# Attention in units of four query tiles, V's scalings and low parts on VectorE, and weights split in three scheduled steps

## The chip, the cores and the metric

The kernel runs on one core of one Trainium2 chip. The metric is the device time of one execution in microseconds (us). The core has TensorE (PE, matrix products and transposes; PEld is its weight load), VectorE (DVE), ScalarE (ACT), GpSimd (POOL) and SyncE (SP, which issues most DMAs). Each engine executes its own instruction list in the order in which the program holds it; semaphores join the lists. Data live in SBUF (128 partitions), sums of matmuls in PSUM banks of 128x512 fp32.

## The reference

The model has two pre-RMSNorm layers on x of 1024 tokens by 1024 features, all float32. Layer 0 is a gated DeltaNet and a gated ConvFFN. Then one K and one V are projected from the stream, and layer 1 is chunked softmax attention on them and a second ConvFFN.

```python
h = h + gated_deltanet(rmsnorm(h, a_norm[0]), ...)
h = h + conv_ffn(rmsnorm(h, f_norm[0]), ...)
kv = rmsnorm(h, kv_norm) @ w_kv                  # 1024 x 2048, K and V of 16 heads of 64
h = h + chunk_attention(rmsnorm(h, b_norm[0]), b_w_q[0], b_rel_bias[0], b_w_out[0], k_pad, v_pad)
h = h + conv_ffn(rmsnorm(h, f_norm[1]), ...)
return rmsnorm(h, final_norm)

def one_chunk(args):                             # 64 queries against a band of 9 chunks of 64 keys
    s = jnp.einsum("bqhd,bkhd->bhqk", q_n, k_band) * scale + bias
    s = jnp.where(valid, s, NEG_INF)
    p = jax.nn.softmax(s, axis=-1)
    return jnp.einsum("bhqk,bkhd->bqhd", p, v_band)
```

## The kernel before

Every fp32 operand of a product is held as a high part (fp32r, `...h` or `whi`) and a low part (what is left, `...l` or `wlo`), and a product is three matmuls: high by high, low by high, high by low (`dense`, L118 to L120). So each operand costs a cast to the high part, mostly on ACT, and a subtraction for the low part, on POOL or DVE.

The program has these stages, in us of the profiled execution: the DeltaNet layer to about 690, FFN 0 to about 1300, the norm and the projection of V to 1411, attention to 1895, FFN 1 to the end. The FFNs and V's projection save matmuls with a scheme of seven products for eight blocks (numbered 1 to 7), whose operands are sums of blocks; each needs its own cast (`uh`, ACT) and subtraction (`ul`).

**The FFN's tail.** Up products go to the PSUM tile `pul`; `vpre`, `gate` and `val` (L1690 to L1696) are the convolution and the gate, `hidh`/`hidl` their product in two parts, `pf` the down product, whose weights are `fr`, `fh` and `fl`. V's weights, tiles `v` of 128x512, are loaded here by SP (L2244).

**V's projection** is `first_halves` with the inner `values()`. Its order is written by hand: `seq` is the list of products and each helper job is put at a place of that list with a rank (`at(i, f, rank)`); the list of every engine follows from it. `fold` scales a tile `v` by the norm's gain (`colt`), `sums` and `left_sum` make the sums of blocks, on the side of the activations (`h`) and of the weights (`v<-v,v`), `highs`/`lows` split the former into `xsum`, `operand` splits the latter into `uh`/`ul`, `product` is 12 matmuls to `pv` (L1475 to L1477), `after` adds products up to `vsum`. The helper `tt` records every `tensor_tensor` there under one line, L1400. Operands of a product are prepared two places ahead of it. The norm ahead of this, `norm_steps`, multiplies `h` by the broadcast factor `psb` (L390), casts `xh` (L393) and subtracts `xl` (L381).

**Attention.** 16 heads are eight pairs p of two heads a; a query tile is 128 queries, a key tile 128 keys, and a query tile sees up to five key tiles (640 keys). For a pair, `kv_tile` projects k and q from weights that are folded (POOL), cast (ACT `whi`, L101) and subtracted (POOL `wlo`, L103); `post_k`, `post_q` and `turn_halves` make the tiles `kA`, `qA`, `qL` and `V`, which hold high and low parts together. Then for one query tile `score` (PE `sc`, L2445/L2446; DVE L2450 adds the bias and finds the maximum; ACT exp L2454; DVE reciprocal L2458; POOL division L2460) leaves the shares `sS`; `turn_run` transposes them (`ptp`, L2505) and splits them into `pTh` (ACT, L2518) and `pTl` (DVE, L2525); `apply_run` multiplies by V into `poT` (L2550/L2551), and the two halves of `poT` are added (ACT `tm` L2556, DVE `oT` L2561). A unit is one head and two query tiles, 64 of them. The out-projection is `acco`.

The order of all engines in attention is made when the program is built, by the list scheduler `Flow` (object `wv`). It keeps a clock T of PE, adds estimated costs of the other engines (`on("D"|"A"|"G", cost)`), and takes at each step the first item by rank whose inputs are ready by that clock; where none is, it places one step of dense work (three matmuls of the next projection, `_dense`). `fetch` loads and splits weights of dense tiles ahead.

Of the kernel before, what the change touches and what calls it, by code (L numbers as in the profile page):

```python
# [9 lines left out]
F32 = mybir.dt.float32  # L10
# [18 lines left out]
def trunk_kernel(  # L29
# [168 lines left out]
    class Flow(Weave):  # L198
# [4 lines left out]
        def __init__(self):  # L203
            super().__init__()
            self.T, self.free, self.aux = 0.0, dict(D=0.0, A=0.0, G=0.0), deque([[0.0], [0.0]])
            self.time, self.items, self.last, self.stalls = {}, [], 0, []
            self.auto, self.tick, self.slack, self.cur, self.nxt, self.units = True, 0, 0.5, None, deque(), 0
            self.brief, self.early, self.split_at, self.hold, self.far = False, 8, 8, None, 4.0

# [60 lines left out]
        def _dense(self):  # L270
            if self.cur is None:
# [3 lines left out]
                if self.nxt[0][1] < 2:  # L275
                    self.stalls.append(self.T)
                    self.T += 3.0 + max(0.0, self.nxt[0][2] + 6.0 - self.T)
                    self.fetch(2)
                e = self.nxt.popleft()
# [69 lines left out]
    def norm_steps(h, s, g, dst, keep=False, gap=False):  # L349
# [29 lines left out]
        def low(t_, k):  # L379
            eng = (nc.gpsimd if k in (0, 1, 2, 3) else nc.vector) if keep and s == 1 else (nc.vector if k % 2 == 0 else nc.gpsimd)  # L380
# [1016 lines left out]
    def values(wts, pss, raw, load, fh, fin, wf, wd, d_vt, more):  # L1397
# [40 lines left out]
        def fold(j, q):  # L1438
# [3 lines left out]
            tt(nc.gpsimd, t_, t_, g, ALU.mult)  # L1442
# [14 lines left out]
        def operand(j, n):  # L1457
# [4 lines left out]
            tt(nc.gpsimd, lo, src, hi.bitcast(F32), sub)  # L1462
# [96 lines left out]
    def ffn(layer, h, hp, xs, tail, d_r, last):  # L1559
# [475 lines left out]
        if layer == 0:  # L2035
# [16 lines left out]
            def closing(s, m):  # L2052
                def f():
                    tt(nc.vector, fh[m][:, hs(s)], fps[s, m], fh[m][:, hs(s)], add)
                    nc.sync.dma_start(out=d_h[m][:, hs(s)], in_=fh[m][:, hs(s)])
                    if m == 0:
                        norms.append(norm_steps(fh, s, None, last, keep=True))
# [229 lines left out]
    with ExitStack() as ph:  # L2287
# [19 lines left out]
        wv.far = 5.79  # L2307

        def kv_tile(src, c0, g, post):
# [5 lines left out]
            wt = split_w(raw, shape, fold=g)  # L2315
            wv.on("G", 3.61, wv.on("A", 0.89, wv.on("G", 2.6)))
# [92 lines left out]
        def bias_tile(hd):  # L2409

            b = bp.tile([P, 640], F32, name="bt", tag="bt", bufs=3)
# [21 lines left out]
        def score(u, kv, a, t, bt):  # L2433
# [14 lines left out]
            S = bp.tile([P, n, w], F32, name="sS", tag="sS", bufs=6)  # L2448
# [17 lines left out]
        units = [(p, *((i % 2, i // 2) if p == 7 else (i // 4, i % 4))) for p in range(8) for i in range(8)]  # L2466
        oTs = {}

        def score_run():
            for p, a, tp in units:  # L2470
# [5 lines left out]
                for i in range(2):  # L2476
                    while live[0] >= 6:
# [4 lines left out]
                    sc.append(score(("S", p, a, tp, i), kvs[p], a, 2 * tp + i, bt))  # L2482
                    yield
                shares.append(sc)
                wv.mark(("sc", p, a, tp), sc_free[0])
                if (a, tp) == (1, 3):
                    wv.mark(("scored", p), sc_free[0])

        def turn_run():
            for p, a, tp in units:  # L2490
                yield from wait(("sc", p, a, tp), *[("S", p, a, tp, i) for i in range(2)])
                sc = shares.popleft()
                kt0, kt1 = sc[0][1], 2 * tp + 1
                blocks = [((kt, 0), (kt, 1)) for kt in range(sc[1][1], 2 * tp + 1)]
                blocks.append(((kt0, 0) if sc[1][1] > kt0 else None, (kt1, 1)))
                for b0 in range(0, len(blocks), 2):
                    bl = blocks[b0 : b0 + 2]
# [3 lines left out]
                    pt = pB.tile([P, 2, 256], F32, name="ptp", tag="pt", bufs=2)  # L2501
                    some = [(j, e) for j, b in enumerate(bl) for e in b if e is not None]
                    for j, e in some:
                        S, s0 = sc[e[1]]
                        nc.tensor.transpose(pt[:, j, e[1] * P : (e[1] + 1) * P], S[:, (e[0] - s0) * P : (e[0] - s0 + 1) * P], ident)  # L2505
                    wv.pe(len(some), 0.15)
                    if b0 + 2 >= len(blocks):
                        live[0] -= 2
                    pTh = bp.tile([P, 2, 256], F32R, name="pTh", tag="pTh", bufs=3)
                    pTl = bp.tile([P, 2, 256], F32R, name="pTl", tag="pTl", bufs=3)  # L2510
                    if bl[-1][0] is None:
                        v = [(0, slice(0, 256)), (1, slice(P, 256))] if len(bl) == 2 else [(0, slice(P, 256))]
                        v = [(pt[:, j, c], pTh[:, j, c], pTl[:, j, c]) for j, c in v]
                    else:
                        n = len(bl)
                        v = [(pt[:, 0:n], pTh[:, 0:n], pTl[:, 0:n])]
                    for s_, h_, l_ in v:
                        nc.scalar.copy(h_, s_)  # L2518
                    t0 = wv.on("A", 0.2 * len(v) + 0.1 * len(some))
                    one = [None, p, a, tp, b0, bl, b0 + 2 >= len(blocks), pTh, pTl]  # L2520
                    pts.append(one)

                    def low(v=v, one=one, slot=slot, n=len(some)):
                        for s_, h_, l_ in v:
                            nc.vector.tensor_tensor(l_, s_, h_.bitcast(F32), op=ALU.subtract)  # L2525
                        one[0] = slot[0] = wv.on("D", 0.08 * len(v) + 0.135 * n)
# [4 lines left out]
        def apply_run():  # L2531
            left = sum(1 for _ in units)
# [343 lines left out]
```

## Time and profile before

| | |
|---|---|
| time, median of 2 runs | 2560.38 us (2556.89 and 2563.86) |
| the profiled execution | 2561.97 us, span 2560.3 us |
| mean granted TensorE clock | 0.991 |
| busy: PE, DVE, ACT, POOL | 2488.0, 1885.7, 1466.9, 1550.6 us |
| 1238 to 1312 (tail of FFN 0): PE busy, clock | 68.41 of 74.00 us, 0.95 |
| 1338 to 1411 (V's products): PE, DVE, POOL busy, clock | 65.30, 36.44, 64.00 of 73.00 us, 0.95 |
| 1472 to 1728 (attention, middle): PE, DVE, ACT, POOL busy, clock | 241.06, 181.21, 172.14, 113.25 of 256.00 us, 0.95 |

A row of a timeline is start, duration, engine, line, operation, result<-inputs, shapes and, in brackets, how long the engine idled before it and what ended that. A row of a group is count, busy time and mean duration in ns, then the idle time of the engine before such instructions. Matmuls overlap, so the time of one is read from the distance of two starts. Half clock shows as starts that lie twice as far apart and as a clock under 1.00.

### The profile page before, as it was taken

The page shows a single profiled execution, that of the slowest core. Times are in us where ns is not written, and L with a number is a line of the kernel's source. Part 1 is how long each engine was busy: PE and PEld are TensorE (multiplying, and loading weights), DVE is VectorE, ACT ScalarE, POOL GpSimd, SP SyncE. Part 2 cuts the span into 40 slices and gives each one's busy share as a digit, 9 for nine tenths or more (in the row PEclk, how much of TensorE's full clock was granted, in tenths as well). Part 3 has the DMA queues.
Part 4 walks back from the last instruction along what each step waited for, and adds up shares of the span by engine and source line. Part 5 has one row for each costly group of instructions (what it writes and reads, how often), then busy time and mean ns, then how long its engine had stood idle before and what let it go on. Part 6 is the DMA issues. An engine that isn't in the chain of part 4 may idle for free.

```text
span 2560.3 us, 39405 instructions
## 1 busy us (share of the span) xinstructions
PE 2488.0 (97%) x13741; PEld 2064.4 (81%) x13741; DVE 1885.7 (74%) x3036; ACT 1466.9 (57%) x2824; POOL 1550.6 (61%) x1533
## 2 busy tenths in 40 slices
PE   8999999999999999999989999999999999999998
PEld 6888888888788888887777788888877887888877
DVE  5765774466888888888674566777579788888886
ACT  6444646554565565655455566666455655666555
POOL 3655553358267777777438444445462777787775
PEclk9999999999999999999999999999999999999999
DMA  8734444555357776668932322222253689877788
GB/s 224 181 107 130 123 130 151 156 176 168 85 121 152 153 145 140 139 142 185 226 97 50 88 57 57 74 60 82 97 157 100 170 158 187 165 168 169 157 185 223
DMA packets 388168, 354.26 MB, mean 138 GB/s; under 512 B 101888, under 2 KB 308736, under 8 KB 387968
## 3 DMA queue, kind: packets, MB, share of 16 engines
q1 hardware_dynamic: 354992, 244.51, 34.0%
q0 software_dynamic: 28224, 98.58, 21.8%
q10 hardware_dynamic: 4752, 8.65, 0.9%
q8 instruction: 108, 1.77, 0.3%
q14 instruction: 92, 0.75, 0.1%
HBM read 182.25 MB, written 156.83 MB: 132 GB/s over the span
## 4 chain that ended last, share of the span: by engine, by line
PE 72%; POOL 7%; DVE 6%; issue 5%; DMA 5%; ACT 2%; SPq 1%; ACTq 0%; POOLq 0%; DVEq 0%
PE pu L1600 7%; PE acc L118 7%; PE acc L119 7%; PE pu L1598 7%; PE pu L1599 7%; PE acc L120 6%; POOL ul L1564 3%; PE pd L1598 3%; PE pd L1600 3%; PE pd L1599 3%; DMA d_rt<-rm 2%; PE acco L118 2%; PE acco L120 2%; PE acco L119 2%; PE ptp L2505 2%
## 5 line engine op out<-in xcount | busy, mean ns | idle before, releaser
L1564 POOL TENSOR_TENSOR ul<-r,uh 128x512 fp32r<-128x512 f32 x266 | 430.2, 1637 | 254.6 <-ACT uh L1586 251.5
L118 PE MATMUL acc<-xh,whi 128*128 128x512 f32 x800 | 333.6, 417 | 0.4 <-ACT xh L1094 0.4
L119 PE MATMUL acc<-xl,whi 128*128 128x512 f32 x800 | 316.2, 395 | 1.7 <-POOL xl L381 1.6
L120 PE MATMUL acc<-xh,wlo 128*128 128x512 f32 x800 | 315.3, 394 | 0.0
L1586 ACT CAST uh<-r 128x512 fp32r<-128x512 f32 x289 | 177.0, 622 | 189.9 <-DVE r L1564 149.8
L103 POOL TENSOR_TENSOR wlo<-wraw,whi 128x256 fp32r<-128x256 f32 (+1 forms) x294 | 216.1, 766 | 99.3 <-ACT whi L101 97.9
L1600 PE MATMUL pu<-xh,ul 128*128 128x512 f32 x524 | 204.7, 391 | 1.7 <-POOL ul L1564 1.7
L1598 PE MATMUL pu<-xh,uh 128*128 128x512 f32 x524 | 204.5, 390 | 0.8 <-ACT keep L1727 0.7
L1954 ACT COPY stage<-pd 128x1024 f32<-128x1024 f32 x180 | 175.3, 1013 | 51.3 <-PE pd L1600 48.7
L1599 PE MATMUL pu<-xl,uh 128*128 128x512 f32 x524 | 204.0, 389 | 0.0
L2460 POOL TENSOR_SCALAR sS<-sS,st 128x640 f32<-128x640 f32 (+4 forms) x128 | 88.0, 691 | 178.3 <-DVE st L2458 146.2
L1693 DVE SCALAR_TENSOR_TENSOR gate<-gpre,colt,gate 128x1023 f32<-128x1023 f32 (+2 forms) x92 | 173.4, 1885 | 11.4 <-ACT gate L1690 10.7
L1564 POOL TENSOR_TENSOR dl<-a,dh 128x512 fp32r<-128x512 f32 x90 | 153.3, 1704 | 46.2 <-ACT dh L1586 37.2
L120 PEld LDWEIGHTS acc<-xh,wlo 128*128 128x128 f32 x800 | 151.4, 189 | 33.4
L119 PEld LDWEIGHTS acc<-xl,whi 128*128 128x128 f32 x800 | 152.4, 191 | 27.0 <-POOL xl L381 4.1
L118 PEld LDWEIGHTS acc<-xh,whi 128*128 128x128 f32 x800 | 152.2, 190 | 24.1 <-ACT xh L1094 0.8
L1693 DVE SCALAR_TENSOR_TENSOR val<-vpre,colt,val 128x1023 f32<-128x1023 f32 x88 | 146.9, 1670 | 33.3 <-ACT val L1690 33.2
L1564 DVE TENSOR_TENSOR r<-r,r 128x512 f32<-128x512 f32 x160 | 130.8, 817 | 35.1 <-POOL ul L1564 33.9
L2450 DVE CUSTOM_DVE_ANT_0 sS<-sc,bt 128x640 f32<-128x640 f32 (+4 forms) x128 | 83.9, 656 | 74.3 <-PE sc L2446 62.8
L1600 PEld LDWEIGHTS pu<-xh,ul 128*128 128x128 f32 x524 | 98.3, 188 | 24.8 <-POOL ul L1564 3.4
L1564 DVE TENSOR_TENSOR el<-val,eh 128x512 fp32r<-128x512 f32 x90 | 86.7, 963 | 43.0 <-ACT eh L1586 43.0
L1598 PEld LDWEIGHTS pu<-xh,uh 128*128 128x128 f32 x524 | 98.4, 188 | 21.7 <-ACT keep L1727 1.1
(456 smaller groups left out, 7504.9 us busy)
## 6 DMA issues: line engine op xcount, KB each, us to landing
r<-in_f_w_up_dram SPq DMA_DIRECT2D x176, 256.0 KB, 4.7
d_r<-stage POOLq DMA_DIRECT2D x78, 512.0 KB, 8.1
d_c<-stage POOLq DMA_DIRECT2D x70, 512.0 KB, 8.6
a<-in_f_w_down_dram SPq DMA_DIRECT2D x72, 256.0 KB, 2.9
wraw<-in_a_w_in_dram SPq DMA_DIRECT2D x32, 512.0 KB, 4.5
d_e<-stage POOLq DMA_DIRECT2D x32, 512.0 KB, 8.6
wraw<-in_a_w_out_dram SPq DMA_DIRECT2D x16, 512.0 KB, 4.2
d_r<-h ACTq DMA_DIRECT2D x32, 256.0 KB, 3.0
```

Of the source, the lines that this page charges most:

```text
L103: nc.gpsimd.tensor_tensor(lo[:, c], raw[:, c], hi[:, c].bitcast(F32), op=ALU.subtract)
L118: mm(ps, hi[:, kw, wcol : wcol + P], rh[k][s], start=st, stop=False)
L119: mm(ps, hi[:, kw, wcol : wcol + P], rl[k][s], start=False, stop=False)
L120: mm(ps, lo[:, kw, wcol : wcol + P], rh[k][s], start=False, stop=sp)
L1564: tt = lambda eng, o, a, b, op: eng.tensor_tensor(o, a, b, op=op)
L1586: copy(hi, src)
L1598: mm(ps, w[0][:, cw], x[0], start=first, stop=False, skip_group_check=True)
L1599: mm(ps, w[0][:, cw], x[1], start=False, stop=False, skip_group_check=True)
L1600: mm(ps, w[1][:, cw], x[0], start=False, stop=last, skip_group_check=True)
L1693: nc.vector.scalar_tensor_tensor(t_[:, a:c1], p_[:, a - step : c1 - step], w[:, 2 - step : 3 - step], t_[:, a:c1], op0=ALU.mult, op1=ALU.add)
L1954: nc.scalar.copy(t_, ps)
L2460: nc.gpsimd.tensor_scalar(S, S, st[:, 3:4], 1.0, op0=ALU.mult, op1=ALU.mult)
```

## The change

1. `norm_steps` gets `odd=True` for the last norm of layer 0: for half 1 the low parts of even tiles are made on DVE and of odd ones on POOL, instead of tiles 0 to 3 on POOL and the rest on DVE.
2. In `values()` the 12 `fold` and the 21 `ul` of `operand` go from POOL to DVE, and the places of `sums`, `highs`, `lows` and `fold` in the list are other ones. The first fold, which stands in the FFN's tail, goes with them.
3. A unit of attention is one head and four query tiles, 32 of them. `banks_of(h)` lists which transposes fill a bank of four 128x128 tiles; the split of a bank is one instruction each on ACT and DVE, and the matmuls of `poT` take 128 to 512 columns at once: 96 each of 128, 256, 384 and 512 in place of 192 of 128 and 384 of 256, the same columns in all. `tm` and `oT` are 64x512, 32 of each instead of 64 of 64x256. `sS` has 7 buffers instead of 6, `bt` (the bias) 2 instead of 3, `tm` 1 instead of 2.
4. `split_later` replaces `split_w` for attention's weights: fold, cast and subtraction become three items that the scheduler places by its clock, and no next dense tile is begun while one is unfinished (`splits`). Two dense tiles are fetched ahead from the start (`brief`, `early = 3`).

Line numbers of the new kernel lie 3 higher up to V's projection and 29 higher in attention's scores.

```diff
-    def norm_steps(h, s, g, dst, keep=False, gap=False):
+    def norm_steps(h, s, g, dst, keep=False, gap=False, odd=False):
...
-            eng = (nc.gpsimd if k in (0, 1, 2, 3) else nc.vector) if keep and s == 1 else (nc.vector if k % 2 == 0 else nc.gpsimd)
+            eng = (nc.gpsimd if k in (0, 1, 2, 3) else nc.vector) if keep and s == 1 and not odd else (nc.vector if k % 2 == 0 else nc.gpsimd)
...
-            tt(nc.gpsimd, t_, t_, g, ALU.mult)
+            tt(nc.vector, t_, t_, g, ALU.mult)
...
-            tt(nc.gpsimd, lo, src, hi.bitcast(F32), sub)
+            tt(nc.vector, lo, src, hi.bitcast(F32), sub)
...
-        for f, n, i in ((sums, 7, 0), (highs, 7, 0), (sums, 6, 1), (highs, 6, 2), (sums, 5, 3), (sums, 4, 4), (highs, 5, 9), (highs, 4, 13)):
+        for f, n, i in ((sums, 7, 1), (highs, 7, 1), (sums, 6, 4), (highs, 6, 4), (sums, 5, 7), (sums, 4, 9), (highs, 5, 11), (highs, 4, 13)):
...
-        for n, i in ((7, 3), (6, 6), (5, 10), (4, 14)):
+        for n, i in ((7, 5), (6, 8), (5, 12), (4, 15)):
...
-        for j, i in ((1, -1), (2, 2), (3, 4)):
-            for q, d in ((11, 0), (12, 1), (21, 4), (22, 5)):
+        for j, i in ((1, 1), (2, 2), (3, 4)):
+            for q, d in ((11, 0), (12, 1), (21, 5), (22, 6)):
...
+        wv.brief, wv.early = True, 3
+        def split_later(raw, shape, fold=None):
+            hi = wp.tile(shape, F32R, name="whi", tag="whi")
+            lo = wp.tile(shape, F32R, name="wlo", tag="wlo")
+            cut = [slice(i * shape[1] // 4, (i + 1) * shape[1] // 4) for i in range(4)]
+            wv.splits += 1
+            def low():
+                for c in cut:
+                    nc.gpsimd.tensor_tensor(lo[:, c], raw[:, c], hi[:, c].bitcast(F32), op=ALU.subtract)
+                wv.on("G", 0.36 * shape[1])
+                wv.splits -= 1
+            def high():
+                nc.scalar.copy(hi, raw)
+                wv.later(wv.on("A", 0.13 * shape[1]), low)
+            if fold is None:
+                high()
+            else:
+                f = fold.rearrange("p (k o) -> p k o", o=1).broadcast_to(shape)
+                for c in cut:
+                    nc.gpsimd.tensor_tensor(raw[:, c], raw[:, c], f[:, c], op=ALU.mult)
+                wv.later(wv.on("G", 2.6), high)
+            return hi, lo
...
-        units = [(p, *((i % 2, i // 2) if p == 7 else (i // 4, i % 4))) for p in range(8) for i in range(8)]
+        units = [(p, *((i % 2, i // 2) if p == 7 else (i // 2, i % 2))) for p in range(8) for i in range(4)]
+        def banks_of(h):
+            if h == 0:
+                return [[(0, 0, 0, 4)], [(3, 0, 3, 1), (1, 1, 1, 3)], [(2, 2, 2, 2)]]
+            return [[(3, 0, 0, 4)], [(4, 0, 0, 4)], [(0, 0, 0, 1), (5, 1, 1, 3)], [(1, 0, 0, 2), (6, 2, 2, 2)], [(2, 0, 0, 3), (7, 3, 3, 1)]]
...
+                for j, (kt, at_, i0, w) in enumerate(bank):
+                    o, c = slice(i0 * P, (i0 + w) * P), slice(at_ * P, (at_ + w) * P)
+                    mm(po[:, o], V[a][:, kt], pTh[:, c], start=n + j == 0, stop=False, skip_group_check=True)
+                    mm(po[:, o], V[a][:, kt], pTl[:, c], start=False, stop=ends and j == len(bank) - 1, skip_group_check=True)
```

**The FFN's tail.** POOL's list at the first fold (`v_13238` is the first tile of V's weights, `fl` and `ul` low parts of the down weights and of an operand of the last up product). Before:

```order
L1564 TENSOR_TENSOR fl_12661<-fr,fh_12660 128x512 [waits DMAHW4_49,Activation_49]
L1564 TENSOR_TENSOR ul<-r_12494,uh 128x512 [waits DMAHW2_49,PE_49,Activation_49]
L1400 TENSOR_TENSOR v_13238<-v_13238,colt 128x512 [waits DMAHW2_49,DMAHW1_49,DVE_49]
L1564 TENSOR_TENSOR fl_12708<-fr,fh_12707 128x512 [waits Activation_49]
L1564 TENSOR_TENSOR ul<-r_12608,uh 128x512 [waits DMAHW3_49,PE_49,Activation_49]
L1400 TENSOR_TENSOR v_13240<-v_13240,colt 128x512 [waits DMAHW4_49,Pool_49]
```

Now the same place of DVE's list, where before `gate` was followed by `vpre` at once:

```order
L1567 TENSOR_TENSOR hidl<-val,hidh 128x1024 [waits DVE_49,Activation_49]
L1696 SCALAR_TENSOR_TENSOR gate<-gpre,colt,gate 128x1022 [waits DVE_49]
L1403 TENSOR_TENSOR v_13238<-v_13238,colt 128x512 [waits DMAHW2_49,DVE_49]
L1567 TENSOR_TENSOR vpre<-pul,keep 128x512 [waits PE_49]
L1567 TENSOR_TENSOR val<-val,gate 128x1024 [waits Activation_49]
L1696 SCALAR_TENSOR_TENSOR val<-vpre,colt,val 128x1023 [waits Activation_49]
L1567 TENSOR_TENSOR hidl<-val,hidh 128x1024 [waits DMASW5_49,DMASW7_49,DMASW4_49,DMAHW0_49,DMASW3_49,Activation_49]
```

The fold has left POOL, where `fl` and `ul` stood behind it, and stands on DVE, where `vpre`, `val` and `hidl` stand behind it.

**V's projection.** DVE's list after the norm, before:

```order
L1400 TENSOR_TENSOR h_12796<-h_12800,h_12796 128x512 [waits Pool_49]
L1400 TENSOR_TENSOR h_12797<-h_12801,h_12797 128x512 [waits Pool_49]
L1400 TENSOR_TENSOR h_12794<-h_12794 128x512 [waits DVE_49]
L1400 TENSOR_TENSOR h_12795<-h_12795 128x512 [waits DVE_49]
L1400 TENSOR_TENSOR h_12796<-h_12796 128x512 [waits DVE_49]
L1400 TENSOR_TENSOR h_12797<-h_12797 128x512 [waits DVE_49]
L1400 TENSOR_TENSOR h_12798<-h_12798,h_12794 128x512 [waits DVE_49]
```

and now:

```order
L1403 TENSOR_TENSOR h_12796<-h_12800,h_12796 128x512
L1403 TENSOR_TENSOR h_12797<-h_12801,h_12797 128x512 [waits DVE_49,Pool_49]
L1403 TENSOR_TENSOR v_13240<-v_13240,colt 128x512
L1403 TENSOR_TENSOR v_13246<-v_13246,colt 128x512
L1403 TENSOR_TENSOR ul<-v_13238,uh 128x512 [waits Activation_49]
L1403 TENSOR_TENSOR v_13248<-v_13248,colt 128x512
L1403 TENSOR_TENSOR ul<-v_13246,uh 128x512 [waits Activation_49]
L1403 TENSOR_TENSOR v_13254<-v_13254,colt 128x512
L1403 TENSOR_TENSOR ul<-v_13240,uh 128x512 [waits Activation_49]
L1403 TENSOR_TENSOR h_12794<-h_12794 128x512
```

Folds and `ul` of the first products stand between the sums of blocks, which come later; DVE's list has 33 operations more there and POOL's as many fewer.

**Attention.** PE's list where a head's later query tiles are transposed and applied (`ptp` transposes, `poT` applies, `sc` scores; dense work is `acc`). Before:

```order
L2550 MATMUL poT<-pTh,V 128x256
L2551 MATMUL poT<-pTl,V 128x256
L2505 MATMUL ptp<-ident,sS 128x128 x3
L2550 MATMUL poT<-pTh,V 128x256
L2551 MATMUL poT<-pTl,V 128x256
L2550 MATMUL poT<-pTh,V 128x256
L2551 MATMUL poT<-pTl,V 128x256
L2445 MATMUL sc<-kA,qA 128x320
L2446 MATMUL sc<-kA,qL_14048 128x320
L2445 MATMUL sc<-kA,qA 128x320
L2446 MATMUL sc<-kA,qL_14048 128x320
```

and now:

```order
L2576 MATMUL poT<-pTl,V 128x512
L2538 MATMUL ptp<-ident,sS 128x128 x8
L2575 MATMUL poT<-pTh,V 128x512
L2576 MATMUL poT<-pTl,V 128x512
L2538 MATMUL ptp<-ident,sS 128x128 x4
L2575 MATMUL poT<-pTh,V 128x128
L2576 MATMUL poT<-pTl,V 128x128
L2575 MATMUL poT<-pTh,V 128x384
L2576 MATMUL poT<-pTl,V 128x384
L2474 MATMUL sc<-kA,qA 128x512
L2475 MATMUL sc<-kA,qL_14442 128x512
```

Eight transposes stand together where three or four did, fewer and wider apply matmuls follow, and no dense matmul stands in this stretch of either list.

More of the change, by code (lines that the diff above doesn't have):

```diff
@@ L2475, in score_run @@
                 sc = []
-                for i in range(2):
-                    while live[0] >= 6:
+                for i in range(4):
+                    while live[0] >= 7:
                         yield wv.T + 0.3
@@ L2481, in score_run @@
                     live[0] += 1
-                    sc.append(score(("S", p, a, tp, i), kvs[p], a, 2 * tp + i, bt))
+                    sc.append(score(("S", p, a, h, i), kvs[p], a, 4 * h + i, bt))
                     yield
                 shares.append(sc)
-                wv.mark(("sc", p, a, tp), sc_free[0])
-                if (a, tp) == (1, 3):
+                wv.mark(("sc", p, a, h), sc_free[0])
+                if (a, h) == (1, 1):
                     wv.mark(("scored", p), sc_free[0])
         def turn_run():
-            for p, a, tp in units:
-                yield from wait(("sc", p, a, tp), *[("S", p, a, tp, i) for i in range(2)])
+            for p, a, h in units:
+                yield from wait(("sc", p, a, h), *[("S", p, a, h, i) for i in range(4)])
                 sc = shares.popleft()
[L2493 to L2497, printed above, removed]
+                banks = banks_of(h)
+                for n, bank in enumerate(banks):
                     while len(pts) >= 3:
@@ L2500, in turn_run @@
                     slot = yield from wv.bank()
[L2501 to L2520, printed above, removed]
+                    pt = pB.tile([P, HALF], F32, name="ptp", tag="pt", bufs=2)
+                    for kt, at_, i0, w in bank:
+                        for i in range(w):
+                            S, s0 = sc[i0 + i]
+                            nc.tensor.transpose(pt[:, (at_ + i) * P : (at_ + i + 1) * P], S[:, (kt - s0) * P : (kt - s0 + 1) * P], ident)
@@ new lines, in turn_run @@
+                    some = sum(w for _, _, _, w in bank)
+                    wv.pe(some, 0.15)
+                    if n == len(banks) - 1:
+                        live[0] -= 4
+                    pTh = bp.tile([P, HALF], F32R, name="pTh", tag="pTh", bufs=3)
+                    pTl = bp.tile([P, HALF], F32R, name="pTl", tag="pTl", bufs=3)
+                    c = slice(min(x[1] for x in bank) * P, HALF)
+                    nc.scalar.copy(pTh[:, c], pt[:, c])
+                    t0 = wv.on("A", 0.2 + 0.1 * some)
@@ L2521, in turn_run, with low @@
+                    one = [None, p, a, h, n, bank, n == len(banks) - 1, pTh, pTl]
                     pts.append(one)
[L2523 to L2526, printed above, removed]
+                    def low(l_=pTl[:, c], s_=pt[:, c], h_=pTh[:, c], one=one, slot=slot, some=some):
+                        nc.vector.tensor_tensor(l_, s_, h_.bitcast(F32), op=ALU.subtract)
+                        one[0] = slot[0] = wv.on("D", 0.08 + 0.135 * some)
@@ L2531, in apply_run @@
         def apply_run():
-            left = sum(1 for _ in units)
+            left = len(units)
             po = None
@@ L2536, in apply_run @@
                     yield wv.T + 0.52
-                t0, p, a, tp, b0, bl, ends, pTh, pTl = pts[0]
+                t0, p, a, h, n, bank, ends, pTh, pTl = pts[0]
                 yield t0
                 V = kvs[p]["v"]
-                if b0 == 0:
-                    yield from wait(*[("v", p, s) for s in range(1 + tp // 2)])
+                if n == 0:
+                    yield from wait(*[("v", p, s) for s in range(1 + h)])
                     while po_free[0] > wv.T:
@@ L2562, in add @@
                         po_free[0] = t = wv.on("D", 0.86)
-                        close(p, a, tp, oT, t)
-                    wv.later(wv.on("A", 0.35), add)
+                        close(p, a, h, oT, t)
+                    wv.later(wv.on("A", 0.6), add)
                 yield
         def close(p, a, tp, oT, t):
-            if p == 7 and a == 1 and tp % 2 == 1:
-                wv.add(1, ("own", tp // 2), wv.when(("acts", tp // 2)), own_act(oT, tp // 2, 7))
-            if p < 7 and (a, tp) == (1, 3):
+            if p == 7 and a == 1:
+                wv.add(1, ("own", tp), wv.when(("acts", tp)), own_act(oT, tp, 7))
```

36 lines of the change are left out of this document (17 added, 19 removed).

## The prediction

> **What bounds the kernel now.** I read the page first, then TensorE's waits by stage, then time by stretches, then the timelines around the longest waits.
>
> ```profile
> PE 2488.0 (97%) x13741; PEld 2064.4 (81%) x13741; DVE 1885.7 (74%) x3036; ACT 1466.9 (57%) x2824; POOL 1550.6 (61%) x1533
> ```
>
> TensorE is busy 97% of the span, so a change of the other engines' work can only win TensorE's waits, the half clock that follows some of them, and narrow matmuls. The change touches three places: the end of FFN 0 (up to 1262 us), V's projection (about 1338 to 1411) and attention (1411 to 1895). TensorE's waits there, one question for each stretch (total us, times, longest):
>
> ```profile
> PE pul L1600 <- POOL ul L1564: 5.6, 1, 5.6
> ...
> PE pv L1477 <- POOL ul L1400: 7.6, 6, 5.6
> PE acc L119 <- POOL xl L381: 1.6, 4, 0.7
> ...
> PE sc L2445 <- DVE st L2450: 16.4, 15, 2.7
> ```
>
> The same stretches as busy time of PE, PEld, DVE, ACT and POOL, then the granted clock:
>
> ```profile
> 1238.00:1312.00 74.00, 68.41 (x296) 56.00 (x295) 45.72 (x55) 34.23 (x61) 18.91 (x14) 0.95 0.67 196
> ...
> 1338.00:1411.00 73.00, 65.30 (x269) 51.18 (x269) 36.44 (x40) 36.57 (x62) 64.00 (x48) 0.95 0.27 58
> ...
> 1472.00:1728.00 256.00, 241.06 (x1424) 212.96 (x1423) 181.21 (x494) 172.14 (x420) 113.25 (x187) 0.95 0.23 62
> ```
>
> A mean clock of 0.95 costs 0.05 of the stretch: 3.7 us, 3.7 us and 12.8 us. The time that could be won is thus 5.6+3.7 in the tail, 7.6+3.7 in the values, and in the five head pairs of 1472 to 1728 the 14.9 us in which PE is idle and those 12.8. All sums below are made against the profiled execution, 2561.97 us, which is 1.6 above the median of 2560.38.
>
> **Part 1, the fold in the FFN's tail.** Rows of SP, POOL, PE and DVE:
>
> ```profile
> 1248.90 0.65 SPq L2244 DMA_DIRECT2D v<-in_w_kv_dram  x1
> ...
> DMA to landing us min/median/max: 5.0/5.0/5.0
> ...
> 1254.11 1.04 POOL L1400 TENSOR_TENSOR v<-v,colt 128x512 f32<-128x512 f32 x1 [10.83 <-DVE val L1693]
> 1255.11 1.26 POOL L1564 TENSOR_TENSOR fl<-fr,fh 128x512 fp32r<-128x512 f32 x1
> 1256.32 1.26 POOL L1564 TENSOR_TENSOR ul<-r,uh 128x512 fp32r<-128x512 f32 x1
> ...
> 1257.64 0.80 PE L1600 MATMUL pul<-xh,ul 128*128 128x512 f32 x1 [5.59 <-POOL ul L1564]
> ...
> 1247.23 0.67 DVE L1564 TENSOR_TENSOR vpre<-pul,keep 128x512 f32<-128x512 f32 x1
> ...
> 1251.57 1.23 DVE L1564 TENSOR_TENSOR hidl<-val,hidh 128x1024 fp32r<-128x1024 f32 x1
> ```
>
> PE's 5.59 us is POOL's queue: the fold stands ahead of the `ul` that PE needs and waits for V's weights, whose load is issued at 1248.90 and lands 5.0 later, at 1253.9 (the row names a DVE operation instead; it ended at about the same time). With the fold on VectorE the `ul` can run at about 1249, so the 5.6 us and the 3.7 of half clock go: −9.3. The same load is now waited for on VectorE, ahead of `vpre`. Queued behind it are `vpre`, two `val` and a `hidl`, and behind those ACT's `val` and `hidh` and PE's eighth matmul of the down product. VectorE comes to the fold at about 1247.2 and leaves it at 1253.9+0.62, so `vpre` is 7.4 us late. What covers this:
>
> ```profile
> 1263.78 1.54 DVE L1693 SCALAR_TENSOR_TENSOR gate<-gpre,colt,gate 128x511 f32<-128x511 f32 x2 [9.80 <-ACT gate L1690]
> ```
>
> VectorE now idles 9.80 us after that group. PE arrives 9.3 earlier, so of the 9.80 there is 0.5 left against 7.4: up to 6.9 us of lateness meet PE, but only at the `hidl` that its eighth down matmul reads, with seven matmuls and then the rest of that product between. By 1256.9 PE is at the first down matmul, by 1258.5 at the eighth; VectorE ends that `hidl` after 1254.5+0.67 and three operations of 1024 columns at 1.23, at 1258.9, hand-overs to ACT aside. I take 1 back. Term: −8, range −9.3 to −2.4.
>
> **Part 2, V's projection.** It moves 12 folds and 21 `ul` from POOL to VectorE; POOL keeps 8 `xsum` lows and 8 `wlo`.
>
> ```profile
> 1335.57 8.59 POOL L1400 TENSOR_TENSOR ul<-v,uh 128x512 fp32r<-128x512 f32 x1 [6.33 <-ACT uh L1461]
> ...
> 1344.21 0.79 PE L1477 MATMUL pv<-xh,ul 128*128 128x512 f32 x1 [5.56 <-POOL ul L1400]
> ...
> 1333.33 2.48 DVE L1400 TENSOR_TENSOR h<-h 128x512 f32<-128x512 f32 x4
> ...
> L1400 POOL TENSOR_TENSOR ul<-v,uh 128x512 fp32r<-128x512 f32 x21 | 36.8, 1757 | 10.6 <-ACT uh L1461 10.6
> L1400 DVE TENSOR_TENSOR v<-v,v 128x512 f32<-128x512 f32 x12 | 16.4, 1372 | 18.0 <-POOL v L1400 18.0
> ```
>
> One POOL `ul` takes 8.59 us, as long as VectorE's run of two-operand sums beside it, and PE waits 5.56 for it. On VectorE an operation of this shape takes 2.48/4 = 0.62 us when POOL stands still, and 1.37 on the mean for `v<-v,v`, when POOL is nearly always busy (64.00 of 73 us). The 33 moved operations at 0.62 add 20.5 us to VectorE's 36.4, 57 in all. PE's own work there is 73 less 7.6 of waits and 3.7 of clock, about 62, so on the mean VectorE fits. Where it is tight: by the new order 39 operations stand from 1333.3 up to the `ul` of the ninth product, 24.2 us, so it is ready at 1357.5. PE, at 12 matmuls of 0.227 a product (the columns' price, below), wants it eight products after 1338.0, where its products begin, at 1359.8. Four POOL `xsum` that could each hold VectorE up for 1.26 (the price of the `fl` above, of the same shape) make it 1362.6, and three hand-overs VectorE, ACT, VectorE of 0.62 each 1364.5. So a new stall of 0 to 4.7; I take 4, near the top, since the hand-overs are certain. The term: −7.6 −3.7 +4 = −7.3, say −7, range −11 to 0 (were a stall of 4 to bring back the half clock too, 3.7 more).
>
> The trace shows that rows of VectorE and POOL lengthen together (8.59; 1.37 against 0.62). The Trainium skill, page "SBUF — State Buffer", section "🔬 SBUF: two separate sides", says that a VectorE operation with two SBUF inputs and a GpSimd operation that reads SBUF share one port pair as an exclusive lock: whichever starts first keeps it and the other fully blocks. The 8.59 us row agrees; the rule speaks against loading VectorE while POOL works, and by it all 16 POOL operations left (at the `fl` row's price some 20 us at most) could come on top, so that the term would be near 0 and the sum about −12.
>
> The norm ahead of it hands POOL four lows of half 1 as before, only other ones: the 1.6 us of `acc` waits may vanish or double, 0 here.
>
> **Part 3, attention.** Rows for the prices:
>
> ```profile
> L2525 DVE TENSOR_TENSOR pTl<-ptp,pTh 128x512 fp32r<-128x512 f32 x80 | 54.9, 686 | 21.7 <-ACT pTh L2518 20.5 <-issue 0.2
> L2525 DVE TENSOR_TENSOR pTl<-ptp,pTh 128x256 fp32r<-128x256 f32 x64 | 26.5, 416 | 0.9 <-ACT pTh L2518 0.7
> L2561 DVE TENSOR_TENSOR oT<-poT,tm 64x256 f32<-64x256 f32 x64 | 27.3, 427 | 5.2 <-ACT tm L2556 3.1
> L2341 DVE TENSOR_TENSOR kA<-acc,kA 64x512 fp32r<-64x512 f32 x32 | 22.0, 689 | 14.9 <-ACT kA L2337 14.4
> ...
> 1566.49 0.28 PE L2551 MATMUL poT<-pTl,V 128*128 128x128 f32 x1
> 1566.61 0.27 PE L2550 MATMUL poT<-pTh,V 128*128 128x128 f32 x1
> ...
> 1562.07 0.28 PE L2551 MATMUL poT<-pTl,V 128*128 128x256 f32 x1
> 1562.19 0.28 PE L2550 MATMUL poT<-pTh,V 128*128 128x256 f32 x1
> ...
> 1565.17 0.39 PE L118 MATMUL acc<-xh,whi 128*128 128x512 f32 x1
> 1565.40 0.39 PE L119 MATMUL acc<-xl,whi 128*128 128x512 f32 x1
> ```
>
> From start to start a 128-wide matmul takes 0.12 like a 256-wide one, a 512-wide one 0.23 (a 384-wide one, by columns, 0.17). Apply goes from 576 matmuls of about 0.115 (66 us) to 96 each of 128, 256, 384 and 512: 96×(0.115+0.115+0.17+0.227) = 60. PE: −6. VectorE: `pTl` 80 to 112 of 686 ns and 64 to 16 of 416, `oT` 64 of 427 to 32 at the price of `kA`, 689: together 12 us less with the 32 smallest `pTl` gone.
>
> Less VectorE work wins only where PE waits for it. The waits now:
>
> ```profile
> 1567.49 1.39 DVE L2356 SCALAR_TENSOR_TENSOR qL<-acc,qA 64x512 fp32r<-64x512 f32 x2
> 1568.89 0.86 DVE L2358 CAST qA<-qA 64x512 fp32r<-64x512 f32 x2
> ...
> 1569.86 0.74 DVE L2386 TENSOR_TENSOR V<-vf,V 128x256 fp32r<-128x256 f32 x2
> 1570.64 0.82 DVE L2450 CUSTOM_DVE_ANT_0 sS<-sc,bt 128x640 f32<-128x640 f32 x1
> ...
> 1571.52 0.63 PE L2445 MATMUL sc<-kA,qA 128*128 128x320 f32 x1 [2.71 <-DVE st L2450]
> 1571.96 0.47 PE L2446 MATMUL sc<-kA,qL 128*128 128x320 f32 x1
> 1572.22 0.47 PE L2445 MATMUL sc<-kA,qA 128*128 128x320 f32 x1
> ...
> 1621.56 0.41 PE L2445 MATMUL sc<-kA,qA 128*128 128x320 f32 x1 [2.68 <-DVE st L2450]
> ```
>
> Once per head pair (the two waits lie 50.0 us apart, so 256 us hold 5.1 pairs), where no dense matmuls are left to fill, VectorE's casts of the next pair stand ahead of a score's operation and PE waits 2.71. The new order has such a stretch per pair, too: five scores, 22 transposes, fourteen apply matmuls and no dense. PE's work in it: 22×0.115 + (6×0.23+8×0.115+6×0.17) + 2×0.23+16×0.145 = 2.5+3.3+2.8 = 8.6 us. VectorE's: 5×0.83 scores, 5×0.686+0.416 `pTl`, 0.69 `oT`, 1.39+0.86+0.74 casts, five reciprocals of a column, a tenth or two each: 12.3. So PE idles about 4 us per pair there, in several pieces, since five scores and six banks of transposes hand over one by one. Before it was (14.9+12.8)/5.1 = 5.4 per pair with the clock. The clock decides: behind the 2.71 us wait the matmuls start 0.26 apart where 320 columns at the 512-wide price take 0.145, so the clock is halved; the 12.8 us are 2.5 a pair. Pieces of 2 us may not bring it on. Per pair, with 6/8 = 0.75 for PE's own saving: 4−5.4−0.75 = −2.1 without a drop, +0.4 with one. I take the middle, −0.8, for five pairs: −4, range −11 to +6 (drops, and an idle time of 5 instead of 4).
>
> On that gate the Trainium skill, page "TensorE: Matmul & The Clock Gate", section "🎯 Why this matters for your kernels", gives no idle gaps over about 3 us as the rule. By it no piece here would drop the clock and the term would be −11; the 2.71 us wait above dropped it, so the measurement decides and I don't take it.
>
> At nothing: the weights split in three steps are the same POOL and ACT instructions, and no wait of PE for `whi` or `wlo` of `acc` stands in the list now; dense work of other tiles hides them. If that cover fails, a PE wait is at most the chain of fold, high and low, a few us a tile. One `tm` buffer and two for the bias are freed a unit ahead of need; a late bias load would cost up to the 5.0 us of the load above per head.
>
> **Sum.** −8 −7 −4 = −19: 2562−19 = 2543 for a profiled run, 2542 beside the median.
>
> **The rivals.** (A) Attention's pieces are short enough and hidden: of 27.7 us two thirds go, −18, and −6 of PE's own: −24−8−9 = −41, 2520. For it: VectorE and ACT are each under three quarters busy there. Against: the 12.5 against 8.6. (B) VectorE is late everywhere: the tail wins 2.4, the values 2, attention 0: −4, 2557. For it: the 0.5 us of cover in the tail, the tie at the ninth product. (C) The other side, slower: VectorE becomes the bound of V's projection, because operations with two SBUF operands take the 1.37 us of `v<-v,v` and not 0.62. It has 84 there, 69 without PSUM: 69×1.37+15×0.69 = 105 us against the stage's 73, +32, less 12 of the other terms: +20, 2580. It is slower than before once the 69 average over (73+12−10)/69 = 1.09 us. Against: `v<-v,v` had POOL at 64 of 73 us beside it, now at most 20.
>
> **Numbers.** Forecast 0.64, A 0.16, B 0.14, C 0.06. The range reaches from A to a little behind B, 2519 to 2560; it leaves out C and the far half of A, and holds each term's bounds taken alone. Two per cent, about what a measurement here can tell from no change, is 51 us: under 2509 only if A and all upper ends meet, 0.03; over 2612 only if C's average exceeds 1.5, 0.01; within 0.96.
>
> **What would show it.** Right: no wait of `pul` for `ul` and full clock near 1257; VectorE's fold waits about 6.7 us at 1247; no 5.6 us wait of `pv`; VectorE near full and POOL mostly idle from 1340 to 1390, with operations of 0.62 to 0.7; PE idle about 4 us per pair. Wrong: `pf` waiting for `hidl` over 2 us; VectorE operations over 1 us in the values; a clock in 1472 to 1728 of 0.99 (A) or under 0.95 (B).

## The result and the profile after

The changed kernel takes 2597.14 us (2593.12 and 2601.15), 1.0149 of the kernel before, interval 1.0121 to 1.0178. The forecast was 2542 with a range to 2560: it is wrong in sign and size. The profiled execution took 2601.15 us with a span of 2599.4. A repeat (experiment 12) gave 2590.95 beside 2555.99 for the kernel before, a ratio of 1.0129 (1.0103 to 1.0155).

The stages, from the starts of their first and last matmuls in the two traces: the FFN's tail (first `pul` to first `pf`) 30.5 us before and 30.7 after; down product, norm and V (first `pf` to last `pv`) 142.6 and 146.9; attention (from there to the last norm sum) 494.4 and 527.3. So attention costs 33 us more and V 4, and the tail won nothing. (The two profiled spans lie 39 us apart. The rest is 4 us less ahead of the tail and 6 more in FFN 1, where this execution holds one wait of 4.3 us that the repeat's trace does not have.)

The page after, PE's share:

```profile
PE 2500.7 (96%) x13549; PEld 2058.8 (79%) x13549; DVE 1895.7 (73%) x2989; ACT 1468.5 (56%) x2744; POOL 1497.2 (58%) x1500
```

Attention as a whole, before and then after (busy time of PE, PEld, DVE, ACT and POOL, then the clock):

```profile
1408.00:1903.00 495.00, 468.99 (x2640) 405.14 (x2639) 329.02 (x820) 304.02 (x700) 238.21 (x359) 0.98 0.30 84
...
1409.00:1936.00 527.00, 476.81 (x2431) 396.49 (x2429) 321.58 (x740) 303.56 (x619) 235.87 (x359) 0.95 0.29 78
```

PE is idle for 26 us there before and for 50 after, and the lower clock takes its share on top. TensorE's waits after, in attention, the tail and V's projection (total us, times, longest):

```profile
PE ptp L2538 <- POOL sS L2489: 19.3, 15, 3.2
PE sc L2474 <- DVE st L2479: 13.1, 25, 3.3
PE ptp L2538 <- DVE pTl L2552: 12.5, 5, 2.5
...
PE pul L1601 <- ACT keep L1758: 6.0, 1, 6.0
...
PE pv L1478 <- DVE vsum L1403: 4.1, 1, 4.1
PE pv L1478 <- ACT uh L1464: 2.4, 1, 2.4
```

The two waits that the change was forecast to remove (`pul` and `pv` for POOL's `ul`) are gone. In their places stand a wait of about the same length for ACT in the tail, two in V's projection, and more waits of the transposes in attention: 19.3 us for POOL's shares, where before it was 0.2, and 12.5 for VectorE's `pTl`, where it was 2.3. The first kind is followed here, the second in experiment 10. The stretches that answer to those before:

```profile
1234.00:1308.00 74.00, 67.96 (x297) 55.56 (x295) 47.47 (x56) 34.08 (x61) 15.96 (x12) 0.95 0.66 197
1334.00:1411.00 77.00, 69.91 (x282) 54.75 (x281) 51.05 (x77) 39.18 (x67) 18.25 (x16) 0.93 0.25 55
1472.00:1728.00 256.00, 230.09 (x1214) 192.93 (x1214) 158.65 (x399) 157.68 (x336) 106.83 (x178) 0.95 0.24 60
```

In attention's middle all five engines are less busy than before, POOL included (106.83 us against 113.25): no engine is the bound, a chain of waits is. POOL's own waits show which:

```profile
POOL bt L2443 <- DMA bt<-in_b_bias_dram: 49.9, 13, 5.7
...
POOL bt L2443 <- DVE st L2487: 6.6, 2, 5.3
```

Before, that group of waits (POOL's memset of a corner of the bias tile `bt`, for the load of that tile) was 5.9 us in 2. One of them, on SP, POOL and PE:

```profile
1637.52 0.33 SPq L2442 DMA_DIRECT2D bt<-in_b_bias_dram  x1
...
1642.22 0.14 POOL L2443 MEMSET bt<- 64x64 f32 x1 [5.56 <-DMA bt<-in_b_bias_dram]
1642.41 0.15 POOL L2444 MEMSET bt<- 64x64 f32 x1
1642.65 1.57 POOL L2489 TENSOR_SCALAR sS<-sS,st 128x640 f32<-128x640 f32 x2
...
1643.51 0.33 PE L2538 MATMUL ptp<-ident,sS 128*128 128x128 f32 x1 [2.14 <-POOL sS L2489]
```

With two bias buffers the load for the next head can be issued only when the last score of the head before the present one has been read; that is where the scheduler puts its request, so the load starts at 1637.5 and POOL, whose list has the memset next, stands until 1642.2. Behind the memset stand the shares of the unit's last two query tiles. All that they need was ready (their reciprocals on VectorE ended by 1639.0), and PE waits for them.

### The profile page after: what moved, and what is told of

Its sections match the earlier page's. It is cut to its first block, busy times and chain, and to the rows that moved or that the text cites. A ratio compares the mean times of both kernels' runs of the same rounds, so it can differ in the third digit from the quotient of the medians.

```text
span 2599.4 us, 38803 instructions
## 1 busy us (share of the span) xinstructions
PE 2500.7 (96%) x13549; PEld 2058.8 (79%) x13549; DVE 1895.7 (73%) x2989; ACT 1468.5 (56%) x2744; POOL 1497.2 (58%) x1500
## 5 line engine op out<-in xcount | busy, mean ns | idle before, releaser
L103 POOL TENSOR_TENSOR wlo<-wraw,whi 128x256 fp32r<-128x256 f32 (+2 forms) x198 | 148.9, 783 | 54.7 <-ACT whi L101 53.3
L1696 DVE SCALAR_TENSOR_TENSOR val<-vpre,colt,val 128x1023 f32<-128x1023 f32 x88 | 148.5, 1687 | 30.9 <-ACT val L1693 30.7
L2552 DVE TENSOR_TENSOR pTl<-ptp,pTh 128x512 fp32r<-128x512 f32 (+1 forms) x128 | 82.2, 652 | 52.5 <-ACT pTh L2546 51.6
```

The costliest lines, as they stand in the source:

```text
L103: nc.gpsimd.tensor_tensor(lo[:, c], raw[:, c], hi[:, c].bitcast(F32), op=ALU.subtract)
L1696: nc.vector.scalar_tensor_tensor(t_[:, a:c1], p_[:, a - step : c1 - step], w[:, 2 - step : 3 - step], t_[:, a:c1], op0=ALU.mult, op1=ALU.add)
```

## The experiments

Ratios are to the kernel before, timed beside each kernel on the same chip. Four chips were used, and the kernel before takes 2555.1 to 2556.3 us on them. A ratio on record can differ from the quotient of the medians by up to 0.0008, which is 2 us, and its interval is 3 to 8 us wide to each side; so where two experiments lie only a few us apart, the traces are read beside the times. The expectations count by the labels of the runs: their first, eighth, ninth, eleventh and twelfth experiments are numbers 1, 6, 7, 9 and 10 here.

**1. The bias tiles made once.**

```diff
-            b = bp.tile([P, 640], F32, name="bt", tag="bt", bufs=2)
-            src = bass.AP(b_bias.tensor, b_bias.offset + hd * 767, [[1, P], [1, 640]])
-            nc.sync.dma_start(out=b, in_=src)
-            nc.gpsimd.memset(b[0:64, 0:64], NEG)
-            nc.gpsimd.memset(b[64:128, 576:640], NEG)
+            b = bt_own[hd % 2]                       # corners set once, ahead of attention
+            src = bass.AP(b_bias.tensor, b_bias.offset + hd * 767 + 64, [[1, 64], [1, 576]])
+            nc.sync.dma_start(out=b[0:64, 64:640], in_=src)
+            nc.sync.dma_start(out=b[64:128, 0:576], in_=src)
```

> The changed kernel, whose two bias tiles are made once: their masked corners are set before attention and never overwritten, the load of each head's bias goes around them in two pieces, and so POOL has no memset to wait for a load with. Theory (two bias buffers: POOL's list waits for the bias load, 49.9 us in 13 waits, with the shares queued behind it): POOL's waits on the load go to zero, PE's 19.3 us of waits for shares fall under 6, one of the two half-clock stretches per head pair goes, and the time is 2568 to 2576 us. Rival (the unit of four itself: its first bank of transposes needs the shares of all four query tiles): POOL's waits go, PE waits for the shares as long, 2590 to 2597.

Measured: 2557.82 us, ratio 1.0008 (0.9995 to 1.0021); 33 us less than the changed kernel's 2590.95. PE's waits for shares are gone from the list, and the other waits stay:

```profile
PE sc L2479 <- DVE st L2484: 14.6, 29, 3.3
PE ptp L2543 <- DVE pTl L2557: 12.5, 5, 2.5
PE pul L1601 <- ACT keep L1758: 5.2, 1, 5.2
PE pv L1478 <- DVE vsum L1403: 4.0, 1, 4.0
```

The same stretch of attention with PE busier and a higher clock:

```profile
1472.00:1728.00 256.00, 236.65 (x1305) 200.29 (x1304) 174.18 (x440) 170.19 (x365) 111.96 (x170) 0.99 0.24 62
```

Half clock begins at 2 places between 1472 and 1728, against 7 in the changed kernel (two in each of three pairs). Attention takes 493.0 us, 34 less. That is 19 of waits and, by the clock rows (0.05 against 0.01 of the stretch), most of the rest half clock behind them. It is more than expected, since half clock behind the other wait of a pair (of a transpose for `pTl`, 2.50 us) came less often, too: in two of five pairs, where the changed kernel has it in four.

**2. Two bias buffers in the kernel before.** The edit is `bufs=3` to `bufs=2` of `bt`.

> The kernel before with two bias buffers in place of three and nothing else. Theory of the bias buffers: POOL waits for the load some 3 to 4 us for most of the 16 heads, PE's waits for shares appear, 2572 to 2585 us. Rival (units of four): under 5 us more, 2558 to 2565.

Measured: 2560.47 us, 1.0026 (1.0012 to 1.0040). POOL waits as in the changed kernel and PE hardly:

```profile
POOL bt L2414 <- DMA bt<-in_b_bias_dram: 53.6, 15, 5.3
...
PE ptp L2505 <- POOL sS L2460: 3.8, 4, 1.9
```

The expectation of the theory missed (some 5 us, not 17 to 30). So two buffers alone are not the cause: POOL standing still for some 50 us costs 5 us where the order leaves distance between a share and its transposes, and 33 where it does not. Both parts are needed: the buffer, and units of four with their transposes close behind the last shares. No run puts two buffers and the memsets under units of four with the old split of the weights, but the traces tell which part of the change took the distance away. From the last share of a head to the first transpose of that unit pass 5.0 us in the kernel before (median of the first 14 heads) and 4.7 with the new split alone (experiment 8); with units of four it is 0.9 with the new split (experiment 1) and 0.6 with the old (experiment 7). Here, in experiment 2, POOL's standing takes it from 5.0 to 2.1, so little reaches PE.

**3. The next head's bias asked for one unit later.** Two buffers and the memsets stay; the request moves to where the second half of a head is scored.

```diff
-        def bias(hd):
-            for n in (hd, hd + 1):
+        def bias(hd, h):
+            for n in (hd, hd + h):
```

> The changed kernel with two bias buffers and their memsets as in it, but the next head's bias is asked for one unit later, when the second half of a head is scored, so that its buffer has long been free and the load can be issued ahead. Theory (what holds POOL up is a load that can only be issued when the head before last has been scored, and not the memset or the number of instructions): POOL's waits on the load fall from 49.9 to under 12 us and the time is that of the first experiment, 2556 to 2564. Rival (any memset behind a load in POOL's list stops it): POOL waits as long, at other places, 2575 to 2597.

Measured: 2563.83 us, 1.0037 (1.0023 to 1.0052); POOL's waits:

```profile
POOL bt L2443 <- DMA bt<-in_b_bias_dram: 11.6, 3, 5.1
```

As the theory had it. What delays POOL is a load that starts late because its buffer comes free late; the memsets, which are all still there, cost little by themselves. The 6 us above experiment 1 stand in the last pair, where heads alternate and the request comes too late again (POOL waits 4.7 us there): a wait of PE for an `xl` of POOL there is 6.4 us, in experiment 1 it is 1.6.

**4. The first scaling out of the tail.** A larger rank puts it behind the first sums of V's projection on VectorE.

```diff
-                at(i + d, lambda j=j, q=q: fold(j, q), 0.5)
+                at(i + d, lambda j=j, q=q: fold(j, q), 2.2 if (j, q) == (1, 11) else 0.5)
```

> The changed kernel with the first scaling of V's weights placed on VectorE behind the first sums of the norm's output, out of the FFN's tail. Theory (VectorE waits for the load, ACT's activation behind it waits for VectorE, the copy that frees PE's bank stands behind that on ACT): PE's 6.0 us wait and 3.4 us of half clock in the tail go, some 9 us less, of which 1 to 2 may come back at the down product or in the values: 2587 to 2590. Rival (the bank's copy was late for another reason): 2595 to 2599.

Measured: 2581.67 us, 1.0107 (1.0092 to 1.0122), 9.3 less than the changed kernel's 2590.95 (5.6 by the ratios); by the traces the tail takes 23.3 us in place of 30.7. Its clock is whole:

```profile
1234.00:1308.00 74.00, 72.44 (x329) 59.40 (x328) 50.65 (x65) 37.90 (x68) 21.96 (x13) 1.00 0.68 203
```

The tail's whole price was the place of one VectorE instruction. In the changed kernel the chain was, on DVE, ACT and PE:

```profile
1250.74 0.69 DVE L1403 TENSOR_TENSOR v<-v,colt 128x512 f32<-128x512 f32 x1 [6.07 <-DMA v<-in_w_kv_dram]
1251.35 0.68 DVE L1567 TENSOR_TENSOR vpre<-pul,keep 128x512 f32<-128x512 f32 x1
...
1252.13 1.24 ACT L1693 ACTIVATE val<-vpre,colt 128x1024 f32<-128x1024 f32 x1 [5.79 <-DVE vpre L1567]
1253.28 0.57 ACT L1758 COPY keep<-pul 128x512 f32<-128x512 f32 x1
...
1253.89 0.79 PE L1601 MATMUL pul<-xh,uh 128*128 128x512 f32 x1 [6.04 <-ACT keep L1758]
```

One load of V's weights is waited for on DVE, so `vpre` is late, so ACT's `val` is late, and behind it in ACT's list stands the copy that PE's next product waits for.

**5. V's part alone**, on the kernel before (parts 1 and 2 of the change).

> The kernel before with the norm's and V's part of the change alone, attention as before. If the stages add up as the two traces show (tail 0, values 4 us longer): 2561 to 2567 us. If VectorE's lateness in the values also delays attention: over 2570. If the forecast's terms hold without the rest: 2545.

Measured: 2556.60 us, 1.0006 (0.9994 to 1.0017), +1.0. That is under the 2561 to 2567 of the stages added up: V's stretch is 3.3 us longer by the trace, but attention, which this edit leaves alone, is 4.9 shorter, with less half clock; why was not looked into. V's part does not explain the loss, and it wins nothing: the tail's wait only moved (PE waits 5.7 for `keep` there), and the `ul` waits gave way to two others.

**6. Experiments 1 and 4 together.**

> The changed kernel with both edits: the bias tiles made once, and the first scaling behind the first sums. If they are independent, 2557.8 of the first alone less the 10 to 12 us that the second won: 2546 to 2549 us, below the kernel before. If the tail's gain is given back where VectorE is late in V's projection: 2555 to 2558.

Measured: 2552.07 us, 0.9984 (0.9971 to 0.9996). Between the two expectations: the second edit wins 5.7 here, not 9.3 to 12. The tail's wait is gone; attention is 2 us longer by its trace (half clock begins at 6 places there instead of 3), so part of it went to the clock.

**7. The old split of the weights**, with the bias tiles of experiment 1 and units of four.

> The changed kernel with the bias tiles made once and the weights split in one go, as before (no split in three steps, no early fetch), units of four kept. If the three-step split is worth what its place in the description suggests: slower than the 2557.8 us of the first experiment, 2565 to 2575, with PE waiting for shares or banks that stand behind folds and low parts on POOL. If it is nothing, as the forecast had it: 2555 to 2560.

Measured: 2562.31 us, 1.0021 (1.0007 to 1.0034), 4.5 more than experiment 1 (3.3 by the ratios, whose intervals overlap; attention is 5.1 longer by the traces). The waits are of another kind:

```profile
PE poT L2581 <- DVE pTl L2557: 11.2, 8, 2.1
```

and half clock begins four times between 1472 and 1728 instead of twice. The three-step split is worth 3 to 5 us here, less than its expectation and more than nothing.

**8. The three-step split alone**, on the kernel before (part 4 of the change).

> The kernel before with the three-step split and the early fetch alone; units of two, three bias buffers, V's part as before. The forecast had this part at nothing: 2552 to 2559 us beside 2555 of the kernel before on this chip. From the ninth experiment, where going back to the old split cost the units of four 4.5 us: 2549 to 2552. If the early fetch disturbs POOL's list: over 2560.

Measured: 2551.36 us, 0.9978 (0.9962 to 0.9994), −5.0. It agrees with the experiment before it. So of the change's parts this one is a gain by itself.

**9. Six of V's low parts back on POOL**, on experiment 6.

```diff
-            tt(nc.vector, lo, src, hi.bitcast(F32), sub)
+            tt(nc.gpsimd if n in (6, 5) else nc.vector, lo, src, hi.bitcast(F32), sub)
```

> The eighth experiment's kernel with six of the 21 low parts of V's projection (products 6 and 5) back on POOL, which is mostly idle there. Theory (VectorE's list is late by the ninth product and frees a bank 4.1 us late): the 4.1 us wait goes, with it one stretch of half clock, 3 to 6 us under the eighth. Rival (POOL's operation with its port contention slows VectorE, 1.3 to 1.8 us each): as the eighth or slower.

Measured: 2548.42 us, 0.9969 (0.9957 to 0.9981), 3.7 less than experiment 6. The 4.1 us wait for `vsum` became two of 2.9 in all, and V's stretch is 4.6 us shorter by the trace. VectorE's list was late there, and POOL could take the work.

**10. The second copy of the queries on POOL**, on experiment 9.

```diff
-                        nc.vector.tensor_copy(qA[a][r2, c], qA[a][r, c].bitcast(F32))
+                        nc.gpsimd.tensor_copy(qA[a][r2, c], qA[a][r, c].bitcast(F32))
```

> The eleventh experiment's kernel with the second copy of the queries (64x512, two per half and pair, 0.42 us each on VectorE) on POOL instead of VectorE. Theory (the 2.5 us that PE waits five times for a transpose bank is VectorE's list, where 2.25 us of the queries' parts stand ahead of a share's low part): each of the five waits falls by 0.8 to 0.9, half clock comes less often, 2542 to 2546 us. Rival (POOL's copies come late for the next scores, or hold VectorE up): 2548 to 2555.

Measured: 2539.38 us, 0.9936 (0.9910 to 0.9962), 9.0 less than experiment 9. The five waits fell from 2.5 to 1.6 each, and half clock is gone from attention's middle:

```profile
PE ptp L2543 <- DVE pTl L2557: 8.2, 5, 1.6
...
1472.00:1728.00 256.00, 240.63 (x1347) 204.16 (x1346) 169.49 (x421) 174.00 (x369) 122.28 (x187) 1.00 0.24 62
```

The waits give back 4.3 us; the rest is mostly the clock (half clock began at four places between 1472 and 1800 in experiment 9, at none here).

**11. Units of two again**, with all else of experiment 10 (and the three bias buffers, memsets and six share buffers of before).

> The twelfth experiment's kernel with units of two query tiles, six share buffers and three bias buffers with memsets as in the kernel before; all else as in the twelfth. If wider apply matmuls and fewer VectorE instructions are worth what the forecast's terms say (6 us of PE, 12 us of VectorE work): 5 to 10 us over the twelfth. If the unit of four gives back in waits what it wins in matmuls: within 3 us of it, 2538 to 2544.

Measured: 2533.45 us, 0.9904 (0.9873 to 0.9934), 5.9 less than with units of four and 22 less than the kernel before: the fastest of all. The ratios' intervals overlap with experiment 10's, but each of its four executions is faster than each of the six there. Its waits in attention:

```profile
PE sc L2474 <- DVE st L2479: 8.1, 12, 2.9
PE poT L2579 <- DVE oT L2590: 4.0, 6, 2.1
...
PE ptp L2534 <- DVE pTl L2554: 1.2, 1, 1.2
```

With units of four (experiment 10) those of the first and last kind were 14.6 and 8.2. What the wider matmuls save, the order gives back in waits, and some more. Attention takes 482.9 us here and 486.5 there. The buffers changed along with the units, so the difference is that of the two together.

**12. The change once more.**

> The changed kernel once more, on the chip of the other experiments. On this chip the kernel before takes 2555 to 2556 us, so at the ratio of 1.0149 the changed one takes 2593 to 2594; if its second bound is the timing of loads that differ between chips, over 5 us away from that.

Measured: 2590.95 us, 1.0129 (1.0103 to 1.0155), with PE's waits for shares at 18.3 us in 15. The loss and the waits came again. (It ran on the chip of experiment 11, not on one chip with all the others, as its expectation says.)

## Why the prediction was wrong, by its own steps

**The step that failed is "At nothing: ... One `tm` buffer and two for the bias are freed a unit ahead of need; a late bias load would cost up to the 5.0 us of the load above per head."** The price was in the text, and 16 heads at up to 5 us are 80 us, but it was neither in the range nor among the rivals. The buffer is free in time for the score that reads it, but not for the request: with two of them, head h+1's is freed by the last score of head h−1, and the request stands at the first score of head h. The prediction asked who waits for the load and thought of the score that reads it. The one that waited was POOL's memset, in the list ahead of shares that had nothing to do with that head. Experiments 1 and 3 show it (−33 and −27 us); experiment 2 shows that it takes the units of four as well.

**Attention, −4.** With the bias wait away it is about +1 by the medians (experiment 1 less experiment 5) and −1.4 by the trace (493.0 against 494.4). Of that the split in three steps, put at nothing, is −4.5 to −5, so the units of four by themselves cost what the split wins: experiments 10 and 11 put them, with their buffers, at +5.9 (+3.6 by attention's traces). The counts were right (96 of each width, 112 `pTl` of 686 ns), the prices of the wider matmuls too (0.11, 0.12, 0.18 and 0.23 us from start to start), and so was the size of the idle time (its sum has twenty apply matmuls where the text says fourteen, which moves little): about 4 us of PE per pair was forecast, and experiment 1's 256 less 236.65 us are 3.8 over 5.1 pairs. What failed is the sum's sign: an order with eight transposes in a row and fewer, larger steps leaves PE waits where units of two had matmuls to go on with.

**The tail, −8.** The load's wait on VectorE came as forecast (6.07 us at 1244.7 to 1250.7) and `vpre` was late; "I take 1 back" was the failing step. Behind `vpre` the prediction counted ACT's `val` and `hidh` and PE's eighth down matmul, but not `keep<-pul` between those two in ACT's list, on which PE's product waits. It cost the whole 6.0 again and the half clock (0.95 in both). Experiment 4 won it back by moving the fold: −9.3 by the times, −7.4 by the tail's traces, −5.7 from experiment 1 to 6, so at most the forecast's gross term of −9.3.

**V's projection, −7.** By experiment 5 tail and V together come to +1.0, by the trace V's stretch to +4. The stall at the ninth product is there as worked out, 2.4 us within the 0 to 4.7. A second of 4.1, at the fifteenth product, is not in the forecast, which followed VectorE's list only to the ninth: a `vsum` that frees a bank stands behind `v`, `ul` and `xsum` there. VectorE is late although it is busy for 51.05 of the 77 us only: it stands 17.0 us in all ahead of its `ul` for ACT's `uh` (first row below), a hand-over that the forecast priced three times at 0.62. The half clock came behind both waits (0.93 of the stretch).

**The rivals.** C had the right sign by the wrong mechanism. VectorE's operations do not take 1.37 us:

```profile
L1403 DVE TENSOR_TENSOR ul<-v,uh 128x512 fp32r<-128x512 f32 x21 | 15.3, 728 | 17.0 <-ACT uh L1464 17.0
...
L1403 DVE TENSOR_TENSOR v<-v,v 128x512 f32<-128x512 f32 x12 | 8.7, 723 | 0.0
```

They take 0.73 and 0.72, far under the 1.09 from which C decides. B's tie at the ninth product and its lost tail came true, and its 2557 is nearly what experiment 1 measured, without the wait for the bias. By its terms it is in part luck: B had −2.4, −2 and 0 for tail, V and attention, and there they came to about −1, +4 and −1. A did not happen.

**The two pages of the Trainium skill.** "SBUF — State Buffer", section "🔬 SBUF: two separate sides" (a VectorE operation with two SBUF inputs and a GpSimd operation that reads SBUF lock each other out): by it V's term was to be near 0, and the stage came to +4, but by queues, as the rows above show; POOL is busy 18.25 us of the 77, so there was little left to be locked out by (VectorE's `xsum` and scalings, some of them beside POOL's, take 0.89 and 0.88). "TensorE: Matmul & The Clock Gate", section "🎯 Why this matters for your kernels" (no idle gaps over about 3 us): waits of 2.50 us were followed by half clock in the changed kernel in most pairs, in experiment 1, at the same length, in two pairs of five, and those of 1.6 us in experiment 10 in none. But in the changed kernel a wait of 1.64 us that ended at 1697.7 was followed by half clock at 1699.2, and one of 3.21 us that ended at 1783.0 was not. So here half clock comes behind waits well under the page's 3 us, and length alone does not decide.

## What to carry to other kernels

A buffer count that goes down is a wait that moves: ask which instruction frees the buffer, where the load's request stands, and which instruction of which in-order list is the first to touch the loaded tile; everything behind that one pays, needed or not. When an instruction with a long wait is moved to another engine's list, follow that list and the lists that wait on it until one reaches the bound engine; a transfer that is late is late in every list. Larger units save instructions and lose the small steps with which a scheduler covers latencies: price both.

## What the runs showed that was not expected

POOL stood still for 53.6 us in experiment 2 and it cost 5 us, and for 49.9 us in the changed kernel and it cost 33: the price of a wait hung on the distance in the order between the late result and its reader (5.0 us against 0.9). Taking 0.85 us off five waits of 2.5 us won 9 us (experiment 10), since the half clock that followed three of them in experiment 9 went, too: in this kernel those waits cost about twice what was taken off them.
